# Tree attention on one core: three output stores one block of loads later, six stores ahead of the last rearranging copies, and one late head stored in 116 and 12 rows

## The chip, the core and the metric

The kernel runs on one core of a Trainium2 chip. The core has a matrix engine (TensorE, PE in the profile, with its weight loads as PEld), three engines for elementwise work (VectorE as DVE, ScalarE as ACT, GpSimd as POOL), a synchronisation engine (SyncE, SP) that here only starts transfers, and 16 DMA engines that move data between HBM and the on-chip memories. A transfer is started by an instruction on POOL, SP or ACT; the profile names the queue q0 for POOL's transfers, q1 for SP's and q10 for ACT's. The metric is the device time of one execution in microseconds (us).

## What is computed

Attention over 96 heads (8 batches of 12) of 512 positions by 64 numbers, in which position i may look only at itself and at its ancestors in a binary tree:

```python
    mask = np.zeros((seq, seq))
    for i in range(seq):
        mask[i, i] = 1
        parent = i
        while parent > 0:
            parent = (parent - 1) // 2
            mask[i, parent] = 1
    scores = np.einsum('bhqd,bhkd->bhqk', Q, K) * scale
    scores = scores + (1 - mask) * (-1e9)
    weights = np.exp(scores - np.max(scores, axis=-1, keepdims=True))
    weights = weights / (np.sum(weights, axis=-1, keepdims=True) + 1e-10)
    return np.einsum('bhqk,bhkd->bhqd', weights, V).astype(np.float32)
```

Q, K, V and the result are float32, 12.58 MB each. Three of them are read and one is written.

## The kernel before

Heads are worked on in 48 pairs (`NP`). For pair i the main loop runs steps named by letters: S computes the scores in two parts on PE (lines 601 to 608 and 635 to 646) and their exponentials on ACT (618 and 652); V multiplies pair i-1's exponentials with V on PE (696) and divides by the sums on DVE (733 and 735), which writes one of the output tiles `of`; K and Q turn the next pairs' keys and queries round with PE transposes (507 to 513 and 566 to 572) and copy the result out of PSUM on DVE (521, 525, 577). Copies at line 374 lay V out in the order that the products need; DVE, ACT and POOL share them.

Loads come in blocks of 8 heads for K and Q (`kst`, `qst`, 512 KB as they land in bf16) and of 16 heads for V (`vst`). A V block arrives as "leaves0" and "leaves1" (256 KB each) and "upper" (512 KB). An output tile `of` holds 8 heads, 1 MB in float32; there are ten of them for twelve blocks of heads. In this text k9 or q9 is the load of K's or Q's heads 72 to 79, leaves(5) that of V's heads 80 to 95, and store 24 the store of heads 24 to 31.

All loads and most stores are issued by POOL, in the order of a list that `pool_program` writes out (line 759). `pool(i)` issues, after pair i's steps, as much from the head of the list as `ready` lets through; nothing overtakes, so an instruction of POOL that waits holds up every load and store behind it. Each transfer of POOL also takes one of eight semaphores in turn, and waits until the transfer eight places before it has landed. Besides transfers the list has POOL's own copies of V's rows (`spread_top`, `spread_pool`, line 374), and `lay_beside` (line 448), a copy of a whole K or Q block of heads 80 to 87 or 88 to 95 into another arrangement, from which PE transposes with half as many instructions (lines 507 and 566).

The list before is made by a loop over blocks. A store goes in once it is `BEHIND` (56) heads and a block behind the loads; what is left is stored after the last load. Heads 72 and 73 are stored by SP after pair 38 in pieces of 116 and 12 rows (`store_apart`, line 753); POOL stores the other six of that block. The last four heads are stored by SP and ACT at the end of the program: pair 46's two heads in halves of 64 rows, one head by each engine, then pair 47's, its first head by SP in halves of 64 rows and its second by ACT in one transfer of 128 rows. One row of one head is 1 KB.

Of the kernel before, what the change touches and what calls it, by code (L numbers as in the profile page):

```python
# [10 lines left out]
CODE = 2048.0  # L11
CODE_ROWS = 40
NOUT = 20
BEHIND = 56

# [104 lines left out]
def kernel(  # L120
# [16 lines left out]
    KB, VB = 8, 16  # L137
# [604 lines left out]
    def store(eng, h0, n, step=1, p0=0, p1=P):  # L742
        return eng.dma_start(  # L743
            out=Or[p0:p1, h0:h0 + step * (n - 1) + 1:step, :],
            in_=ofs[h0 // 8][p0:p1, h0 % 8:h0 % 8 + step * (n - 1) + 1:step, :, :].rearrange(
                "p h t d -> p h (t d)"
            ),
        )


    APART, APART_AT, APART_ROWS = 72, 38, 116
# [7 lines left out]
    def pool_program():  # L759

        ops = [
            (load_k, 2, 2), (load_q, 2, 2), (load_v, 0, 4), (load_v, 4, 4),
            (load_k, 4, 2), (load_k, 6, 2), (load_q, 4, 2), (load_k, 8, 4),
            (load_q, 6, 2), (load_q, 8, 4), (load_v, 8, 8), (load_k, 12, 4),
            (load_q, 12, 4), (load_k, 16, 4), (load_rows, 1, "upper"),
            (load_q, 16, 4), (load_rows, 1, "even"), (load_k, 20, 4), (load_rows, 1, "odd"),
            (load_q, 20, 4), (load_k, 24, 8), (load_q, 24, 4), (load_rows, 2, "upper"),
            (load_q, 28, 4), (load_rows, 2, "leaves0", "leaves1"), (load_k, 32, 8), (load_q, 32, 8),
            (load_rows, 3, "upper"),
            (spread_pool, (1, "Z0", 8, 16), (1, "Z1", 8, 16), (1, 6, 8, 16), (1, 9, 8, 16)),  # L770
            (load_q, 40, 8), (load_k, 40, 8), (load_rows, 3, "leaves0", "leaves1"), (load_k, 48, 8),
            (spread_top, 2), (spread_pool, (2, "Z0", 0, 16), (2, "Z1", 0, 16)), (load_q, 48, 8),
            (spread_pool, (2, "X", 0, 16), (2, "M", 0, 16), (2, "D1", 0, 16)), (spread_top, 3, 0, 12),
            (load_rows, 4, "upper"), (spread_top, 3, 12, 16),
        ]
        loaded, stored = 72, 0
        for h in range(56, NH, KB):
            top = [(spread_top, h // VB + 0)] if h % VB == 8 and 4 <= h // VB + 0 < NH // VB else []
            if top:
                top.append((spread_pool, (h // VB, "Z0", 0, 16), (h // VB, "Z1", 0, 16)))  # L780
            ops += [(load_k, h, KB)] + top + [(load_q, h, KB)]
            if h == 64:
                ops.append((
                    spread_pool, *[(3, part, 0, 16) for part in ("Z0", "Z1", "X", "M", "D1")]
                ))
            while loaded < min(h + 32, NH):
                names = ("leaves0", "leaves1") if loaded % VB else ("upper",)
                ops.append((load_rows, loaded // VB) + names)
                loaded += KB
            if top:  # L790
                o = h // VB
                ops.append((spread_pool, *[(o, part, 0, 16) for part in ("X", "M", "D1")]))
            if stored + KB + BEHIND <= h + KB:
                ops.append((store, nc.gpsimd, stored, KB))
                stored += KB
        ops.insert(-1, (lay_beside, "kst", 80 // KB))
        while stored < NH - KB:
            n = 2 if stored == APART else 0
            ops.append((store, nc.gpsimd, stored + n, KB - n))
            if stored == 40:  # L800
                ops.append((lay_beside, "qst", 80 // KB))
            if stored == 64:
                ops += [(lay_beside, "kst", 88 // KB), (lay_beside, "qst", 88 // KB)]
            stored += KB
        ops += [(store, nc.gpsimd, NH - KB + h, 2) for h in (0, 4)]
        return ops

# [57 lines left out]
    def spread_by(copy, table, steady, i):  # L865
# [34 lines left out]
    for i in range(NP + 1):  # L900
        steps = FIRST[i] if i < len(FIRST) else "SVK" if i % 2 else "SVQ"
        if i >= max(FAR, KFAR - 4):
            steps = ("SVK", "SVQ", "SVK", "SQV")[i % 4]
        elif i == FAR - 1:
            steps = "SQVK"
        for step in steps:
            if step == "S" and i < NP:
                scores1(i)
                scores2(i)
            if step == "V" and i >= 1:  # L910
                values(i - 1)
# [12 lines left out]
            if step == "D":  # L924
                spread_by(nc.vector.tensor_copy, BY_VECTOR, STEADY_VECTOR, i)
            if step == "A":
                spread_by(nc.scalar.copy, BY_SCALAR, STEADY_SCALAR, i)
        if "D" not in steps:
            spread_by(nc.vector.tensor_copy, BY_VECTOR, STEADY_VECTOR, i)
        if "A" not in steps:  # L930
            spread_by(nc.scalar.copy, BY_SCALAR, STEADY_SCALAR, i)
        pool(i)
        if i == APART_AT:
            store_apart()
        if i == NP - 1:
# [37 lines left out]
```

## Time and the profile before

| | |
|---|---|
| median of 3 runs | 132.93 us (132.81 to 133.04) |
| the profiled execution, its own time | 132.49 us |
| its span, first to last instruction | 130.7 us |
| busy: PE, DVE, ACT, POOL | 113.7, 105.6, 101.1, 84.4 us |
| read from HBM, written to HBM | 37.94 MB, 12.58 MB |

The profile is of one execution. 1.8 us of its time lie outside the span. A load counts in the DMA rates with the bytes that land (bf16), a store with what it writes (float32), so 200 GB/s of loads and 400 GB/s of stores are about the same traffic at HBM. "Landing" is when the last part of a transfer has reported.

### The profile page before, as it was taken

What the parts mean: (1) busy time and instruction counts of PE and PEld (TensorE: products, weight loads), DVE (VectorE), ACT (ScalarE), POOL (GpSimd) and SP (SyncE); (2) the same over time, 40 slices, a digit from 0 to 9 for tenths busy, and PEclk for the clock granted to TensorE, in tenths of its full rate; (3) what the DMA queues carried; (4) which work ended last, traced back from release to release, by engine and by line L of the source; (5) the groups of instructions that cost most, each with busy time, mean ns of one, the idle gap of its engine ahead of it and who ended that gap; (6) DMA issues with size and microseconds to landing.
All of it is one profiled execution on the core that took longest, in us unless ns stands there. A gap on an engine that the chain in (4) does not pass through costs nothing.

```text
span 130.7 us, 5436 instructions
## 1 busy us (share of the span) xinstructions
PE 113.7 (87%) x2353; PEld 81.0 (62%) x2353; DVE 105.6 (81%) x254; ACT 101.1 (77%) x163; POOL 84.4 (65%) x116
## 2 busy tenths in 40 slices
PE   6688969999799887899998999896999997999940
PEld 2354755766577566677776786674677675776630
DVE  3349779888999998989998998987898997894560
ACT  4179676989779995968987799797689785889930
POOL 6999625354483999995299899953999963202130
PEclk9999999999999999999999999999999999999995
DMA  2999999999999999999999999999999999999984
GB/s 89 248 190 192 201 195 201 201 202 205 201 203 208 208 205 207 208 210 205 207 211 201 283 292 210 270 309 231 338 228 322 257 277 397 402 404 386 382 339 145
DMA packets 26071, 32.25 MB, mean 247 GB/s; under 512 B 1240, under 2 KB 19544, under 8 KB 26048
## 3 DMA queue, kind: packets, MB, share of 16 engines
q0 software_dynamic: 24384, 30.41, 111.4%
q1 hardware_dynamic: 944, 0.91, 2.2%
q10 hardware_dynamic: 720, 0.59, 1.5%
q8 instruction: 18, 0.29, 0.8%
q14 instruction: 5, 0.04, 0.1%
HBM read 37.94 MB, written 12.58 MB: 386 GB/s over the span
## 4 chain that ended last, share of the span: by engine, by line
DVE 29%; DMA 28%; PE 22%; POOL 7%; ACT 6%; issue 4%; ACTq 0%; DVEq 0%; POOLq 0%
DMA vst<-in_V_dram 17%; DMA qst<-in_Q_dram 11%; DVE of L735 9%; PE ob L696 8%; DVE vt L374 6%; PE s L601 3%; DVE qq L577 3%; ACT e L652 3%; DVE rec L733 3%; DVE kk L521 3%; POOL kst L247 2%; PE s L608 2%; DVE kk L525 2%; POOL qst L247 2%; ACT e L618 2%
## 5 line engine op out<-in xcount | busy, mean ns | idle before, releaser
L618 ACT ACTIVATE e<-s 128x1024 bf16<-128x1024 f32 x40 | 40.9, 1024 | 15.0 <-PE s L608 14.6
L696 PE MATMUL ob<-vt,e 128*128 128x65 bf16 (+1 forms) x940 | 37.1, 197 | 2.6 <-DVE of L735 1.0
L696 PEld LDWEIGHTS <-e 128*128 128x128 bf16 (+1 forms) x960 | 30.1, 102 | 9.6 <-DVE of L735 1.9
L374 POOL COPY vt<-vst 32x512 int32<-32x512 int32 (+4 forms) x44 | 32.5, 739 | 4.7 <-PE ob L696 2.5
L652 ACT ACTIVATE e<-s 128x384 bf16<-128x384 f32 x80 | 34.7, 490 | 0.0
L735 DVE TENSOR_TENSOR of<-ob,rec 128x512 f32<-128x512 f32 x47 | 32.5, 691 | 1.6
L374 DVE COPY vt<-vst 32x1024 bf16<-32x1024 bf16 (+5 forms) x47 | 20.9, 445 | 2.8 <-DMA vst<-in_V_dram 1.9
L743 POOL DMA_DIRECT2D out_dram<-of x13 | 11.5, 888 | 12.9 <-DVE of L735 12.4
L733 DVE RECIPROCAL rec<-ob 128x8 f32<-128x8 f32 x47 | 9.5, 202 | 9.9 <-PE ob L696 9.3
L257 POOL DMA_DIRECT2D kst<-in_K_dram x11 | 8.0, 725 | 7.4 <-DMA qst<-in_Q_dram 3.2
L601 PE MATMUL s<-far,codes 40*128 40x512 bf16 x64 | 12.5, 386 | 0.0
L635 PEld LDWEIGHTS <-codes 40*128 40x128 bf16 x80 | 6.2, 94 | 8.7 <-issue 3.9
L614 ACT ACTIVATE e<-s 128x1024 bf16<-128x1024 f32 x8 | 8.2, 1023 | 4.1 <-PE s L608 4.0
L577 DVE COPY qq<-qtp 128x1024 bf16<-128x1024 bf16 x16 | 10.9, 680 | 0.3 <-PE qtp L572 0.3
L635 PE MATMUL s<-far,codes 40*128 40x384 bf16 x64 | 10.7, 324 | 0.4 <-ACT e L652 0.2
L257 POOL DMA_DIRECT2D qst<-in_Q_dram x12 | 8.5, 708 | 3.8 <-DMA vst<-in_V_dram 1.9
L374 ACT COPY vt<-vst 32x512 int32<-32x512 int32 (+3 forms) x19 | 10.4, 545 | 0.4
L608 PE MATMUL s<-qq,kk 64*128 64x512 bf16 x48 | 9.2, 378 | 1.0 <-DVE qq L577 1.0
L646 PEld LDWEIGHTS <-kk 64*128 64x128 bf16 x192 | 8.4, 94 | 2.6
L521 DVE COPY kk<-ktp 128x256 bf16<-128x256 bf16 x24 | 9.0, 414 | 0.7 <-PE ktp L513 0.7
L302 POOL DMA_DIRECT2D vst<-in_V_dram x7 | 5.6, 800 | 6.0 <-DMA vst<-in_V_dram 4.3
L572 PE MATMUL qtp<-ptile,qst 128*64 128x128 bf16 x192 | 7.5, 221 | 1.7 <-DVE qq L577 1.0
(64 smaller groups left out, 178.2 us busy)
## 6 DMA issues: line engine op xcount, KB each, us to landing
out_dram<-of POOLq DMA_DIRECT2D x10, 1024.0 KB, 15.2
kst<-in_K_dram POOLq DMA_DIRECT2D x9, 512.0 KB, 16.5
qst<-in_Q_dram POOLq DMA_DIRECT2D x8, 512.0 KB, 14.8
vst<-in_V_dram POOLq DMA_DIRECT2D x12, 256.0 KB, 13.5
vst<-in_V_dram POOLq DMA_DIRECT2D x6, 512.0 KB, 12.9
qst<-in_Q_dram POOLq DMA_DIRECT2D x6, 256.0 KB, 12.1
kst<-in_K_dram POOLq DMA_DIRECT2D x4, 256.0 KB, 10.3
out_dram<-of POOLq DMA_DIRECT2D x1, 768.0 KB, 13.0
```

The costliest lines, as they stand in the source:

```text
L257: return nc.gpsimd.dma_start(out=kept[b][:, h0 % KB:h0 % KB + n, :, :].rearrange("p (g x) t d -> p g (x t d)", x=x), in_=src[:, h0 // x:(h ...
L374: return copy(out=dst, in_=src)
L521: nc.vector.tensor_copy(out=columns(flat, 32 * unit, (640, 4), (step, 2), (4, 8), (1, 4)), in_=columns(kp, base, (256, 4), (128, 2), (1, 8 ...
L577: nc.vector.tensor_copy(out=qqs[j][:, :, 8 * last:8 * last + 8, :].rearrange("p b u c -> p b (u c)"), in_=quarters,)
L601: nc.tensor.matmul(out=sp[:, a, :], lhsT=(k1code if i < WIDE else k1wide)[64 * a:64 * a + CODE_ROWS, :], rhs=(q1code, q1wide, q1far)[(i >= ...
L608: nc.tensor.matmul(out=sp[:, a, :], lhsT=keys(i, a, TOP), rhs=qTs[i][64 * a:64 * a + 64, :, :].rearrange("p t c -> p (t c)"), start=False, ...
L618: ) if i < WIDE else nc.scalar.activation(
L635: nc.tensor.matmul(out=flat[:, a, :, :].rearrange("p u (t c) -> p u t c", t=4)[:, :, :, 32 // n:], lhsT=k2wide[64 * a:64 * a + CODE_ROWS, ...
L652: nc.scalar.activation(out=e2s[i % NE][:, a, :, 32:128].rearrange("p t (r u) -> p t r u", u=n), in_=flat[:, a, :, :].rearrange("p u (t r) ...
L696: nc.tensor.matmul(out=ob[lo:hi, a, 65 * t:65 * t + 65], lhsT=e[:, a, PLACE[t], lo:hi], rhs=vt[vtile[tile_v][0]][:, head(i, a) % VB, vtile ...
L733: nc.vector.reciprocal(out=rec[:, a:a + n, :, :], in_=o4[:, a:a + n, :, D:D + 1])
L735: nc.vector.tensor_tensor(out=ofs[j][:, h0:h1 + 1:head(i, 1) - head(i, 0), :, :], in0=o4[:, a:a + n, :, 0:D], in1=rec[:, a:a + n, :, :].to ...
```

## The change

The loop over blocks is replaced by a list that is written out, `BEHIND` goes, and SP's store of pair 46's first head is cut differently. Loads, copies and stores are the same ones as before; in POOL's order four things move:

- stores 8, 16 and 24 each come one block of loads later: store 8 after the loads of k9 and q9 and not before them, store 16 after k10 and q10, store 24 after k11, q11, POOL's last copies of V and the two `lay_beside` of heads 80 to 87;
- the load upper(5) comes after k8, q8, POOL's copies for V block 3 and leaves(5), and not ahead of store 0;
- the second `lay_beside` of heads 80 to 87 (of `qst`) follows the first directly, ahead of every store of that stretch;
- stores 24 to 64, six in a row, stand ahead of the two `lay_beside` of heads 88 to 95.

POOL before, from the load upper(5) to that of k9. `of_312` is the output tile of heads 0 to 7, `of_597` of 8 to 15, `of_875` of 16 to 23; `vst_1914` is V block 5, and the `kst` and `qst` rows are k8, q8 and k9:

```order
L302 DMA vst_1914<-in_V_dram 64x16x256
L743 DMA out_0_dram<-of_312 128x8x256
L257 DMA kst_1917<-in_K_dram 128x2x1024
L257 DMA qst_1919<-in_Q_dram 128x2x1024
L374 COPY vt1_1_122<-vst_822 32x32x32 x2
L374 COPY vt1_2_123<-vst_822 32x32x32 x2
L374 COPY vt1_1_122<-vst_822 32x8x2x32
L293 DMA vst_1914<-in_V_dram 32x8x512 x2
L743 DMA out_0_dram<-of_597 128x8x256
L257 DMA kst_1929<-in_K_dram 128x2x1024
```

POOL after, at the same place; V block 5 is `vst_1924` here, k8 and k9 are `kst_1468` and `kst_1928`:

```order
L742 DMA out_0_dram<-of_312 128x8x256
L256 DMA kst_1468<-in_K_dram 128x2x1024
L256 DMA qst_1470<-in_Q_dram 128x2x1024
L373 COPY vt1_1_122<-vst_822 32x32x32 x2
L373 COPY vt1_2_123<-vst_822 32x32x32 x2
L373 COPY vt1_1_122<-vst_822 32x8x2x32
L292 DMA vst_1924<-in_V_dram 32x8x512 x2
L301 DMA vst_1924<-in_V_dram 64x16x256
L256 DMA kst_1928<-in_K_dram 128x2x1024
```

The upper rows of V block 5 have moved from the front to behind the leaves, and the store of heads 8 to 15 (`of_597`) no longer stands between leaves(5) and k9.

POOL before, around the rearranging copies of line 448, from the load of q11 (`qst_2466`) on; `kst_2007` and `qst_2009` are k10 and q10, `kst_2268` is k11, and the output tiles are those of heads 32 to 71 in order:

```order
L257 DMA qst_2466<-in_Q_dram 128x2x1024
L374 COPY vt1_2_123<-vst_1914 32x32x32 x2
L374 COPY vt1_1_122<-vst_1914 32x8x2x32
L448 COPY kst_2536<-kst_2007 128x1024
L743 DMA out_0_dram<-of_1443 128x8x256
L743 DMA out_0_dram<-of_1701 128x8x256
L448 COPY qst_2540<-qst_2009 128x1024
L743 DMA out_0_dram<-of_1984 128x8x256
L743 DMA out_0_dram<-of_2244 128x8x256
L743 DMA out_0_dram<-of_2512 128x8x256
L448 COPY kst_2784<-kst_2268 128x1024
L448 COPY qst_2786<-qst_2466 128x1024
```

POOL after, at the same place; `of_1151` is the output tile of heads 24 to 31:

```order
L256 DMA qst_2465<-in_Q_dram 128x2x1024
L373 COPY vt1_2_123<-vst_1924 32x32x32 x2
L373 COPY vt1_1_122<-vst_1924 32x8x2x32
L447 COPY kst_2535<-kst_2006 128x1024
L447 COPY qst_2537<-qst_2008 128x1024
L742 DMA out_0_dram<-of_1151 128x8x256
L742 DMA out_0_dram<-of_1444 128x8x256
L742 DMA out_0_dram<-of_1711 128x8x256
L742 DMA out_0_dram<-of_1983 128x8x256
L742 DMA out_0_dram<-of_2243 128x8x256
L742 DMA out_0_dram<-of_2511 128x8x256
L447 COPY kst_2784<-kst_2267 128x1024
```

The store of heads 24 to 31 has come down into this stretch, both copies for heads 80 to 87 stand ahead of it, and all six stores stand ahead of the copies for heads 88 to 95.

SP before, its stores: two heads apart, then pair 46's first head and pair 47's first head:

```order
L743 DMA out_0_dram<-of_2769 116x256 x2
L743 DMA out_0_dram<-of_2769 12x256 x2
L743 DMA out_0_dram<-of_3206 64x256 x4
```

SP after:

```order
L742 DMA out_0_dram<-of_2769 116x256 x2
L742 DMA out_0_dram<-of_2769 12x256 x2
L742 DMA out_0_dram<-of_3206 116x256
L742 DMA out_0_dram<-of_3206 12x256
L742 DMA out_0_dram<-of_3206 64x256 x2
```

Pair 46's first head goes out as rows 0 to 115 and rows 116 to 127; ACT's stores and pair 47's stay as they were. The diff, without the lines that only define names:

```diff
-            if stored + KB + BEHIND <= h + KB:
-                ops.append((store, nc.gpsimd, stored, KB))
-                stored += KB
-        ops.insert(-1, (lay_beside, "kst", 80 // KB))
-        while stored < NH - KB:
-            n = 2 if stored == APART else 0
-            ops.append((store, nc.gpsimd, stored + n, KB - n))
-            if stored == 40:
-                ops.append((lay_beside, "qst", 80 // KB))
-            if stored == 64:
-                ops += [(lay_beside, "kst", 88 // KB), (lay_beside, "qst", 88 // KB)]
-            stored += KB
...
+        ops += k7 + q7 + leaves(4) + out(0)
+        ops += k8 + q8 + [(spread_pool, *[(3, part, 0, 16) for part in ("Z0", "Z1", "X", "M", "D1")])]
+        ops += leaves(5) + [(load_rows, 5, "upper")]
+        ops += k9 + tops(4) + q9 + rest(4) + out(8)
+        ops += k10 + q10 + out(16)
+        ops += k11 + tops(5) + q11 + rest(5)
+        ops += [(lay_beside, "kst", 80 // KB), (lay_beside, "qst", 80 // KB)]
+        for h in range(24, 72, KB):
+            ops += out(h)
+        ops += [(lay_beside, "kst", 88 // KB), (lay_beside, "qst", 88 // KB)]
+        for h in range(72, NH - KB, KB):
+            n = 2 if h == APART else 0
+            ops += out(h + n, KB - n)
...
         if i == NP - 1:
-            for p in (0, P // 2):
-                for a, eng in enumerate((nc.sync, nc.scalar)):
-                    store(eng, head(i - 1, a), 1, 1, p, p + P // 2)
+            for part in range(2):
+                for a, (eng, p) in enumerate(((nc.sync, 116), (nc.scalar, P // 2))):
+                    store(eng, head(i - 1, a), 1, 1, *((0, p), (p, P))[part])
```

More of the change, by code (lines that the diff above doesn't have):

```diff
@@ L13 @@
 NOUT = 20
-BEHIND = 56
 UNITS = (
@@ L775, in pool_program @@
         ]
[L776 to L792, printed above, removed]
-            if stored + KB + BEHIND <= h + KB:
-                ops.append((store, nc.gpsimd, stored, KB))
-                stored += KB
@@ L796, in pool_program, with tops @@
-        ops.insert(-1, (lay_beside, "kst", 80 // KB))
-        while stored < NH - KB:
-            n = 2 if stored == APART else 0
-            ops.append((store, nc.gpsimd, stored + n, KB - n))
-            if stored == 40:
-                ops.append((lay_beside, "qst", 80 // KB))
-            if stored == 64:
-                ops += [(lay_beside, "kst", 88 // KB), (lay_beside, "qst", 88 // KB)]
-            stored += KB
+        def tops(o):
+            return [(spread_top, o), (spread_pool, (o, "Z0", 0, 16), (o, "Z1", 0, 16))]
@@ new lines, in rest, with out, leaves, qk @@
+        def rest(o):
+            return [(spread_pool, (o, "X", 0, 16), (o, "M", 0, 16), (o, "D1", 0, 16))]
+        def out(h0, n=KB):
+            return [(store, nc.gpsimd, h0, n)]
+        def leaves(o):
+            return [(load_rows, o, "leaves0", "leaves1")]
+        def qk(h0):
+            return [(load_k, h0, KB)], [(load_q, h0, KB)]
+        k7, q7 = qk(56)
+        k8, q8 = qk(64)
+        k9, q9 = qk(72)
+        k10, q10 = qk(80)
+        k11, q11 = qk(88)
+        ops += k7 + q7 + leaves(4) + out(0)
```

## Prediction

> **What bounds the kernel now.** I read the page's head and its row of DMA slices first:
>
> ```profile
> span 130.7 us, 5436 instructions
> ...
> DMA  2999999999999999999999999999999999999984
> ```
>
> From the second slice to the 38th no slice of the DMA row is below 9: taken together the DMA engines never run out of work. So I read the stretches of the end next, with one of the middle for comparison (columns: stretch, its length, busy time and instructions of PE, PEld, DVE, ACT, POOL, the clock, the DMA engines' share, and what they moved in GB/s):
>
> ```profile
> core 0: us, PE busy (x) PEld busy (x) DVE busy (x) ACT busy (x) POOL busy (x), PEclk, DMA share, GB/s
> ...
> 80.00:90.00 10.00, 9.23 (x212) 6.88 (x211) 8.89 (x20) 8.24 (x14) 6.76 (x8) 1.00 1.13 261
> ...
> 114.00:120.00 6.00, 5.76 (x108) 4.08 (x109) 4.46 (x10) 5.18 (x10) 0.00 (x0) 1.00 1.03 402
> 120.00:124.00 4.00, 3.87 (x84) 2.60 (x80) 1.80 (x4) 3.81 (x7) 0.89 (x1) 1.00 0.96 373
> ...
> 127.00:128.00 1.00, 0.00 (x0) 0.00 (x0) 0.00 (x0) 0.00 (x0) 0.00 (x0) 0.58 0.88 279
> 128.00:129.00 1.00, 0.00 (x0) 0.00 (x0) 0.00 (x0) 0.00 (x0) 0.00 (x0) 0.50 0.88 262
> 129.00:130.00 1.00, 0.00 (x0) 0.00 (x0) 0.00 (x0) 0.00 (x0) 0.00 (x0) 0.50 0.21 67
> ```
>
> Stores run at 402 GB/s while all engines have work, 25.1 per DMA engine. From 120 on the rate falls, though stores are queued: some of the 16 have run dry, others have not. After 127.0 all compute is over and only transfers are left. Which engines have work to the end shows in the POOL stores' issue times (each row was asked for by itself, so each is one store) and, in the same order, their times to landing:
>
> ```profile
> 102.68 1.10 POOL L743 DMA_DIRECT2D out_dram<-of  x1
> ...
> 103.78 0.89 POOL L743 DMA_DIRECT2D out_dram<-of  x1
> ...
> 104.66 0.89 POOL L743 DMA_DIRECT2D out_dram<-of  x1
> ...
> 111.56 0.83 POOL L743 DMA_DIRECT2D out_dram<-of  x1 [1.61 <-DVE of L735]
> ...
> 120.25 0.89 POOL L743 DMA_DIRECT2D out_dram<-of  x1 [7.86 <-DVE of L735]
> ...
> 124.72 0.72 POOL L743 DMA_DIRECT2D out_dram<-of  x1
> ```
>
> ```profile
> out_dram<-of POOLq DMA_DIRECT2D x1, 1024.0 KB, 14.0
> ...
> out_dram<-of POOLq DMA_DIRECT2D x1, 1024.0 KB, 16.3
> ...
> out_dram<-of POOLq DMA_DIRECT2D x1, 1024.0 KB, 18.0
> ...
> out_dram<-of POOLq DMA_DIRECT2D x1, 768.0 KB, 13.0
> ...
> out_dram<-of POOLq DMA_DIRECT2D x1, 1024.0 KB, 6.9
> ...
> out_dram<-of POOLq DMA_DIRECT2D x1, 256.0 KB, 3.8
> ```
>
> Sums: landings at 116.7, 120.1, 122.7, 124.6, 127.2 and 128.5. A landing is that of the last engine's part. From 120.1 on the steps are 2.6, 1.9, 2.6 and 1.3 for 1024, 768, 1024 and 512 KB (two stores of 256), which is 402 GB/s each time (1,049 KB / 402 = 2.61). So the engine that lands last works without a gap at full pace up to 128.5, while the total rate says that others already idle. The step before, 116.7 to 120.1, is 3.4, that is 0.8 longer than a store needs. In that store something made other engines the last ones.
>
> **The 116-row pieces.** SP's queue q1 had two of them in flight then, 256 KB with their 12-row pieces. Its rows for 108 to 114 and 114 to 120.7, and for 127 to 128, where it carries 64-row pieces:
>
> ```profile
> q1 hardware_dynamic: 156, 0.14, 6.7%
> ...
> q1 hardware_dynamic: 132, 0.12, 5.2%
> ...
> q1 hardware_dynamic: 129, 0.11, 34.6%
> ```
>
> In 116-row pieces the queue moved 0.26 MB in 12.7 us (20 GB/s), busy for about 6% of 16 engines, one engine's worth. In 64-row pieces it moved 0.11 MB in 1 us (110 GB/s) at 35%, five times as much, although POOL's and ACT's queues were also at work. So a 116-row piece is carried by a few engines: between a fifth and a quarter of them by that ratio. I take a quarter, four engines with 29 rows each. An even spread over 16 would have lengthened each of the stores of that time by 20/402, 0.13 us; one step of 0.8 in a single store and none after fits four engines that were ahead, took 58 KB each (2.3 us at 25.1 GB/s), used up their lead and came out last.
>
> The Trainium skill, "DMA: Bandwidth & Descriptors", section "Why a DMA increments its semaphore by 16 and not by 1", gives the rule: a transfer from SP or ACT uses the largest number of engines up to 16 that divides its slowest dimension, and the lowest-numbered ones. By it 116 rows go to four engines, 12 rows to twelve and 64 rows to all, and the sum below would be the same to a tenth; the rows above agree with four, and no row here names the engines.
>
> **The change, part by part.**
>
> Stores 8, 16 and 24 behind k9/q9, k10/q10, k11/q11, and upper(5) behind k8/q8: each load has 1 MB (or upper(5)'s 512 KB, the same traffic at HBM) less ahead of it in q0 and lands 2.6 us earlier. What that is worth to compute is PE's wait for loads between 78 and 96, and no more:
>
> ```profile
> PE ktp L513 <- DMA kst<-in_K_dram: 1.2, 2, 1.0
> PE qtp L572 <- DMA qst<-in_Q_dram: 0.7, 2, 0.5
> ```
>
> 1.9 us at most. DVE, 8.9 us busy in ten there, keeps some, so I take 1.3. The last division then ends 1.3 earlier than the 126.97 below. But bytes are not saved: an engine that is busy to 128.5 without a gap has the same work in another order. For the end this part is worth 0 by itself, up to -1.3 if the issue of the last stores were the bound.
>
> ```profile
> 126.55 0.42 DVE L735 TENSOR_TENSOR of<-s,rec 128x256 f32<-128x256 f32 x1
> ...
> 125.67 2.46 SPq L743 DMA_DIRECT2D out_dram<-of  x4
> ...
> out_dram<-of SPq DMA_DIRECT2D x1, 64.0 KB, 3.0
> ```
>
> SP's last issue ends at 128.13 and begins some 0.6 earlier (2.46 / 4), at 127.5; the last bytes move soon after 129 (67 GB/s in that row). A piece of 64 rows took up to 3.0 us (SP's first). So the path of the issues and the drain of the last engine end close together today; the first moves forward by 1.3, the second does not.
>
> Late stores: does anything wait for them? Of the ten output tiles two are used again, those of stores 0 and 8, for heads 80 to 95. Store 8 goes ahead of k10 in q0, and heads 80 on are computed from k10. Nothing.
>
> Upper(5) later, with its issue, its landing and its first reader:
>
> ```profile
> 58.73 0.83 POOL L302 DMA_DIRECT2D vst<-in_V_dram  x1
> ...
> vst<-in_V_dram POOLq DMA_DIRECT2D x1, 512.0 KB, 17.1
> ...
> 90.23 4.87 POOL L374 COPY vt<-vst 32x512 int32<-32x512 int32 x6 [2.49 <-PE ob L696]
> ```
>
> It landed at 75.8. Store 0, k8, q8 and leaves(5) now go ahead of it, four times 2.6, so 86.2. POOL's copies that read it began at 90.2 and would begin near 89: almost 3 us of cover, 0. Without it q11, which POOL issues behind these copies, would come late, and the copies for heads 88 to 95 next.
>
> Both copies for heads 80 to 87 first, then six stores, then the copies for heads 88 to 95:
>
> ```profile
> 101.70 1.05 POOL L448 COPY qst<-qst 128x1024 int32<-128x1024 int32 x1
> 102.68 2.86 POOL L743 DMA_DIRECT2D out_dram<-of  x3
> 106.43 1.04 POOL L448 COPY kst<-kst 128x1024 int32<-128x1024 int32 x1 [0.89 <-DMA kst<-in_K_dram]
> 108.91 1.04 POOL L448 COPY qst<-qst 128x1024 int32<-128x1024 int32 x1 [1.43 <-DMA qst<-in_Q_dram]
> ```
>
> Q's copy ended at 102.75 with two stores ahead of it; without them (0.95 each, 2.86 / 3) it ends at 100.9, or a little before. Six stores take POOL to 106.6, the two copies to 108.7. They waited for k11 and q11 until 106.4 and 108.9; those now land 2.6 earlier, so the stores, not the loads, set them. PE needs the two results one after the other:
>
> ```profile
> 110.13 0.61 PE L507 MATMUL ktp<-ptile,kst 128*128 128x128 bf16 x8
> ```
>
> With compute 1.3 ahead that is 108.8 for K and about 111 for Q. K's copy is done at 107.6. Cost 0, with 1.2 us of cover; without it every later pair would slip. q0 meanwhile has q11 until 106.3 and stores 24 and on behind it, so no gap opens there.
>
> Pair 46's first head in 116 and 12 rows: before, 64 + 64 rows, 8 KB on each of 16 engines. After, 29 + 1 KB on each of four. Those four gain 22 KB, the others lose 7 or 8. At 25.1 GB/s per engine that is +0.88 us. With a fifth of the engines (39 KB each) it is +1.24. At the rate of 128 to 129 (262 GB/s over 88% of 16, 18.6 per engine) it is +1.18. From below: if the four were not the last, the end would be 8 KB earlier, -0.32. I take +0.95, near the 402 GB/s row, since the last landings kept that pace to the end.
>
> Sum: 0 + 0 + 0.95. The profiled execution's 132.49 becomes 133.44 (span 131.65); the median of the runs lies 0.44 above that execution, so 132.93 + 0.95 = 133.9.
>
> **Rivals.** A difference of 0.2%, 0.27 us, is about what a measurement of this kernel can tell from none.
>
> (a) The four engines are not the last. Place: the last landing. Price -0.32, 132.6. It decides if their lead over the others at 128.5 is 0.9 us or more. For it: the fall of the rate from 120 on shows engines with a lead, and the issue path, 1.3 earlier, would no longer stand in the way. Against it: the step of 0.8 at 120.1. The same page, section "Latency and other measured facts", says that engines 7 and 15 are usually slower; if those were the last, this is the case, but no row here shows single engines.
>
> (b) The issue of the last stores bounds the end, not the drain. Then compute's 1.3 us comes through: 131.6. Against it: the landings without a gap, and 279 and 262 GB/s after the last compute.
>
> (c) Both cancel: the four had half a microsecond in hand, and the result lies within 0.27 of 132.9.
>
> (d) Slower still: the 116 rows start late in their queue. SP issued the first 116-row store at 104.3, and in the stretch 104 to 108 the only queue with bytes was q0:
>
> ```profile
> 104.30 0.27 SPq L743 DMA_DIRECT2D out_dram<-of  x1
> ...
> q0 software_dynamic: 434, 1.09, 110.2%
> ```
>
> If the 29 rows per engine run alone at half pace, +1.8, or POOL's six stores delay the copies for heads 88 to 95, 2 us and more. 134.7.
>
> **Chances.** Forecast (+0.5 to +1.3) 0.62, (d) 0.08, (c) 0.12, (a) 0.11, (b) 0.07. Slower by over 0.2%: 0.70. Same: 0.12. Faster: 0.18. The forecast's own range is 133.4 to 134.2; for 8 in 10 it reaches down to (a) without most of it and all of (b), and up into (d): 132.4 to 134.6.
>
> **What would show it.** The span is about 131.7; the last microsecond before the end has some 100 GB/s (four engines at 25) where 67 stood in 129 to 130, and q1 rather than q10 carries it. PE's waits for `kst` and `qst` between 78 and 96 fall under 0.6, and the last division ends between 125 and 126. The copies for heads 88 to 95 follow a store directly, without a wait for DMA. Wrong would be: a DMA rate of zero within 129.5 of the start, which is (a) or (b); PE waiting for `kst` or `qst` on line 507 or 566, which is (d).

## The result and the profile after

The changed kernel took 133.74 us (median of 6 runs, 133.34 to 133.80), the kernel before 132.87 us beside it (6 runs, 132.60 to 133.04). The ratio is 1.0063, with a 95% interval of 1.0046 to 1.0080: 0.84 us slower, between 0.61 and 1.06. The forecast was 133.9.

The page of the changed kernel: its head, the row of the DMA slices, and the group of DVE's copies of V (before: 20.9 us, 445 ns each).

```profile
span 132.0 us, 5436 instructions
...
DMA  3999999999999999999999999999999999999982
...
L373 DVE COPY vt<-vst 32x1024 bf16<-32x1024 bf16 (+5 forms) x47 | 23.1, 492 | 2.9 <-DMA vst<-in_V_dram 2.1
```

The DMA engines are as full as before. What differs is the end. The stretches of the end of the changed kernel, with the columns of the prediction's table:

```profile
114.00:120.00 6.00, 5.76 (x111) 4.08 (x107) 4.46 (x11) 5.18 (x10) 0.00 (x0) 1.00 1.03 402
120.00:124.00 4.00, 3.87 (x80) 2.60 (x78) 1.84 (x5) 3.81 (x7) 0.89 (x1) 1.00 0.98 383
...
127.00:128.00 1.00, 0.00 (x0) 0.00 (x0) 0.06 (x1) 0.00 (x0) 0.00 (x0) 1.00 0.78 214
128.00:129.00 1.00, 0.00 (x0) 0.00 (x0) 0.00 (x0) 0.00 (x0) 0.00 (x0) 0.52 0.96 263
129.00:130.00 1.00, 0.00 (x0) 0.00 (x0) 0.00 (x0) 0.00 (x0) 0.00 (x0) 0.50 0.55 181
130.00:131.00 1.00, 0.00 (x0) 0.00 (x0) 0.00 (x0) 0.00 (x0) 0.00 (x0) 0.50 0.09 30
```

The rate while all engines have work is the same 402 GB/s. In 127 to 128 it is lower than before (214 where 279 stood), and the bytes come afterwards: 181 GB/s in 129 to 130 where 67 stood, and 30 beyond 130, where the kernel before had moved its last. Who moves these bytes stands in the queues' rows for 129 to 131 (packets, MB, share of 16 engines), in the changed kernel:

```profile
q1 hardware_dynamic: 130, 0.10, 16.0%
q10 hardware_dynamic: 127, 0.11, 15.9%
```

and in the kernel before:

```profile
q1 hardware_dynamic: 65, 0.05, 7.9%
q10 hardware_dynamic: 21, 0.02, 2.4%
```

Only SP's stores (q1) were cut differently, but ACT's (q10) are late as well. ACT's two halves of pair 46's second head take longer from issue to landing, after:

```profile
out_dram<-of ACTq DMA_DIRECT2D x1, 64.0 KB, 4.4
...
out_dram<-of ACTq DMA_DIRECT2D x1, 64.0 KB, 4.2
```

where before they took

```profile
out_dram<-of ACTq DMA_DIRECT2D x1, 64.0 KB, 3.1
...
out_dram<-of ACTq DMA_DIRECT2D x1, 64.0 KB, 2.9
```

A landing is that of the last engine's part, and one number hides the others. The trace also keeps the single steps in which a store's semaphore (the counter that tells when it has landed) rises. They show how many engines carry a piece: a piece of 64, 112 or 128 rows rises in 16 separate steps, one of 116 rows in four, one of 12 rows in twelve and one of 127 rows in one, and what is missing to 16 comes all at once near the issue. Read as one step per engine, the last store of the program, SP's last 64 rows, tells when each of the 16 was done (us from the start of the span; the span ends 0.9 after the last one in every row):

| kernel (the lower ones are the experiments below) | the twelve that end first | the last four |
|---|---|---|
| before | 129.40 to 129.70 | 129.70, 129.71, 129.77, 129.81 |
| changed | 129.44 to 130.05 | 130.27, 130.47, 130.91, 131.06 |
| e1_order | 128.57 to 129.33 | 129.49, 129.76, 129.87, 130.23 |
| e2_rows | 128.93 to 129.43 | 129.94, 130.16, 130.32, 130.62 |
| e3_rows112 | 129.63 to 129.99 | 130.03, 130.05, 130.09, 130.33 |
| e4_rows_both | 130.23 to 130.70 | 131.73, 131.89, 131.90, 132.51 |
| e5_apart_even | 127.69 to 128.84 | 128.95, 129.06, 130.02, 130.19 |
| e6_before_apart_even | 129.86 to 130.21 | 130.23, 130.26, 130.51, 131.27 |
| e7_stores_back | 130.49 to 130.87 | 130.89, 130.89, 130.89, 130.96 |
| e10_rows127 | 131.22 to 131.71 | 131.80, 131.93, 132.36, 135.46 |

Before, all 16 end within 0.4 us. In the changed kernel the first twelve end up to 0.35 us later than before, and the last four 0.6 to 1.25 us later. ACT's halves land late because these four carry their sixteenths of them too: of the first half twelve parts are in by 128.90 and four come at 129.43 to 130.15.

Compute's part: in the changed kernel PE's list of waits between 78 and 96 holds no load any more (columns: us in total, times, longest). It is headed by

```profile
PE s L607 <- DVE qq L576: 0.4, 1, 0.4
PE ob L695 <- DVE of L734: 0.2, 1, 0.2
```

and POOL's stores, its copies for heads 88 to 95, and the last division stand in the changed kernel's timeline (start, length) as

```profile
101.19 5.31 POOL L742 DMA_DIRECT2D out_dram<-of  x6
...
106.49 1.05 POOL L447 COPY kst<-kst 128x1024 int32<-128x1024 int32 x1
107.47 1.05 POOL L447 COPY qst<-qst 128x1024 int32<-128x1024 int32 x1
...
126.63 0.42 DVE L734 TENSOR_TENSOR of<-s,rec 128x256 f32<-128x256 f32 x1
```

The copies follow the stores without a wait. But the last division is where it was before (126.55): in this execution the 1.9 us that PE no longer waits for loads did not reach the end of compute.

### The profile page after: what moved, and what is told of

Same layout as the page of the kernel before. It is cut to its first block, busy times and chain, and to the rows that moved or that the text cites. A ratio compares the mean times of both kernels' runs of the same rounds, so it can differ in the third digit from the quotient of the medians.

```text
span 132.0 us, 5436 instructions
## 1 busy us (share of the span) xinstructions
PE 114.3 (87%) x2353; PEld 81.0 (61%) x2353; DVE 107.5 (81%) x254; ACT 101.1 (77%) x163; POOL 84.4 (64%) x116
## 4 chain that ended last, share of the span: by engine, by line
DVE 39%; PE 24%; DMA 19%; POOL 6%; ACT 4%; issue 3%; ACTq 0%; POOLq 0%
DVE of L734 12%; DMA qst<-in_Q_dram 12%; PE ob L695 9%; DMA vst<-in_V_dram 7%; DVE vt L373 7%; DVE kk L520 5%; DVE qq L576 5%; DVE kk L524 5%; PE s L600 3%; DVE rec L732 3%; PE s L607 2%; POOL kst L246 2%; POOL qst L246 2%; ACT e L617 2%; ACT e L651 2%
## 5 line engine op out<-in xcount | busy, mean ns | idle before, releaser
L617 ACT ACTIVATE e<-s 128x1024 bf16<-128x1024 f32 x40 | 40.9, 1024 | 15.0 <-PE s L607 14.6
L373 DVE COPY vt<-vst 32x1024 bf16<-32x1024 bf16 (+5 forms) x47 | 23.1, 492 | 2.9 <-DMA vst<-in_V_dram 2.1
L645 PE MATMUL s<-qq,kk 64*128 64x160 bf16 (+1 forms) x192 | 8.9, 208 | 0.0
```

The source lines that it names most:

```text
L373: return copy(out=dst, in_=src)
L617: ) if i < WIDE else nc.scalar.activation(
L645: nc.tensor.matmul(out=flat[:, a, :, lo:hi], lhsT=keys(i, a, WTILE2[t]), rhs=qT[64 * a:64 * a + 64, :, lo:hi], start=False, stop=t == 1, s ...
```

## The experiments

The theory, as the prediction had it: the end is set by the DMA engines, the one that lands last; the uneven cut puts 22 KB more on each of four of them and costs all of the loss; the new order on POOL is worth nothing at the end. The first rival was that both parts contribute; later ones were that a lead of the four engines, or the end of compute, decides. Each kernel was timed in turns with the kernel before on the same chip. All of them, with the ratio to the kernel before and its 95% interval, and the difference worked out from it and the median of before on that chip (132.75 us for e1 to e4, 133.0 for e5 to e8, 133.11 for e9 to e12). On the second and third chip the kernel before was itself spread over more than 1.4 us, and plain medians give other differences there (+0.72, +0.56 and +0.61 for e5, e6 and e7; -0.32, -0.42 and -0.18 for e8, e9 and e12), so that a tenth or two decides nothing between these rows:

| kernel | median us | ratio | difference, us |
|---|---|---|---|
| e1_order: new order on POOL, halves of 64 rows | 133.23 | 1.0036 [1.0016, 1.0056] | +0.48 |
| e2_rows: order before, 116 + 12 rows | 133.58 | 1.0064 [1.0046, 1.0083] | +0.85 |
| e3_rows112: order before, 112 + 16 rows | 132.84 | 1.0004 [0.9986, 1.0021] | +0.05 |
| e4_rows_both: order before, both heads of pair 46 in 116 + 12 | 135.21 | 1.0186 [1.0161, 1.0210] | +2.47 |
| e5_apart_even: changed kernel, heads 72 and 73 in 112 + 16 | 133.72 | 1.0043 [1.0013, 1.0072] | +0.57 |
| e6_before_apart_even: kernel before, heads 72 and 73 in 112 + 16 | 133.56 | 1.0032 [1.0005, 1.0060] | +0.43 |
| e7_stores_back: stores 8 to 24 and upper(5) moved, second copy behind three stores | 133.61 | 1.0031 [0.9999, 1.0064] | +0.41 |
| e8_copies_first: only the second copy moved | 132.68 | 0.9961 [0.9936, 0.9986] | -0.52 |
| e9_first_92: e8 and heads 72 and 73 in 92 + 36 | 132.69 | 0.9975 [0.9949, 1.0001] | -0.33 |
| e10_rows127: order before, 127 + 1 rows | 138.34 | 1.0395 [1.0347, 1.0444] | +5.26 |
| e11_less_compute: kernel before with less copying | 132.83 | 0.9982 [0.9956, 1.0009] | -0.24 |
| e12_copies_first_again: e8 a second time | 132.93 | 0.9979 [0.9953, 1.0006] | -0.28 |

**One part alone: the order (e1_order) and the rows (e2_rows).** e1 is the changed kernel with pair 46 in halves again; e2 is the kernel before with the uneven cut.

```diff
 e1_order, against the changed kernel
-            for part in range(2):
-                for a, (eng, p) in enumerate(((nc.sync, 116), (nc.scalar, P // 2))):
-                    store(eng, head(i - 1, a), 1, 1, *((0, p), (p, P))[part])
+            for p in (0, P // 2):
+                for a, eng in enumerate((nc.sync, nc.scalar)):
+                    store(eng, head(i - 1, a), 1, 1, p, p + P // 2)
 e2_rows, against the kernel before: the same lines the other way round
```

> POOL's new order alone, pair 46's first head in two halves of 64 rows as before. Drain theory (the engine that drains last has the same work in any order): ratio to before 1.000, between 0.998 and 1.001. Rival (the path of the last issues bounds the end and late stores help): 0.990. Rival (the order itself costs, through vector copies that take longer beside POOL's copies: the mean of line 373's DVE copies went from 445 to 492 ns in the changed kernel): 1.003 or more.

> The old order, with pair 46's first head stored in 116 and 12 rows. Drain theory: all of the loss, ratio 1.0065 (0.87 us), between 1.005 and 1.008, and the last landings show q1 alive for about a microsecond after the rest. Rival (the cut costs nothing and the order costs): 1.000.

The rows alone cost 0.85 us [0.61, 1.10], as much as the whole change. In e2's trace the end is the expected one in part: four engines are done 0.5 to 1.2 us after the twelfth (129.94 to 130.62 against 129.43), but SP's queue is not the only one alive then, since the four have their share of ACT's stores left as well. The order alone, which was to cost nothing, cost 0.48 us [0.21, 0.74]. The two don't seem to add up: 0.48 + 0.85 is 1.33, and the whole change cost 0.84. The gap of 0.49 is about as large as the three intervals together leave room for. It fits an end that is a maximum over engines and not a sum of delays. The end of e1_order, in the same columns:

```profile
127.00:128.00 1.00, 0.00 (x0) 0.00 (x0) 0.00 (x0) 0.00 (x0) 0.00 (x0) 0.50 0.98 329
128.00:129.00 1.00, 0.00 (x0) 0.00 (x0) 0.00 (x0) 0.00 (x0) 0.00 (x0) 0.50 0.64 215
129.00:130.00 1.00, 0.00 (x0) 0.00 (x0) 0.00 (x0) 0.00 (x0) 0.00 (x0) 0.50 0.12 41
```

and its last division, with its last but one and its last POOL store:

```profile
125.55 0.42 DVE L734 TENSOR_TENSOR of<-s,rec 128x256 f32<-128x256 f32 x1
...
119.25 0.89 POOL L742 DMA_DIRECT2D out_dram<-of  x1 [7.87 <-DVE of L734]
...
123.72 0.72 POOL L742 DMA_DIRECT2D out_dram<-of  x1
```

```profile
out_dram<-of POOLq DMA_DIRECT2D x1, 1024.0 KB, 8.3
...
out_dram<-of POOLq DMA_DIRECT2D x1, 256.0 KB, 5.2
```

Here compute does end 1.0 us earlier, the stores are issued 1.0 earlier, and more bytes move in 127 to 128 (329 where 279 stood). Yet the landings, 119.25 + 8.3 = 127.55 and 123.72 + 5.2 = 128.9, are 0.4 later than before (127.2 and 128.5), while most engines are done earlier: twelve of the 16 by 129.33, where before they took until 129.70, and the last at 130.23 against 129.81. So a few engines fell behind somewhere. Which, and why, the trace does not tell.

**Is it the number of rows or the unequal cut? (e3_rows112, e10_rows127, e4_rows_both)** In all three the order is that of the kernel before and only the cut of pair 46 differs.

```diff
-                for a, eng in enumerate((nc.sync, nc.scalar)):
+                for a, (eng, p) in enumerate(((nc.sync, 112), (nc.scalar, P // 2))):   e3_rows112
+                for a, (eng, p) in enumerate(((nc.sync, 127), (nc.scalar, P // 2))):   e10_rows127
+                for a, (eng, p) in enumerate(((nc.sync, 116), (nc.scalar, 116))):      e4_rows_both
```

> The old order, with that head stored in 112 and 16 rows: as unequal as 116 and 12, but both numbers divide by 16. Theory that a piece is carried by as many engines as divide its rows: 8 KB on each of 16 engines as with the halves, ratio 1.000. Rival (a large first piece ahead of a small one in SP's queue costs, however it is spread): 1.005 or more.

> The old order, with pair 46's first head in 127 rows and 1 row. Theory of divisors (127 has none up to 16 but 1): one engine carries 127 KB and 1 KB where it had 8, 120 KB more, 4.8 us at 25.1 GB/s if that engine was among the last: ratio 1.033 to 1.040; at the 18.6 GB/s of the last stretch 6.5 us, 1.049. Rival (pieces that do not divide by 16 go through four engines or so): 1.007.

> The old order, with both heads of pair 46 stored in 116 and 12 rows, SP's and ACT's. Drain theory: the same four engines get 22 KB more twice, 1.76 us at 25.1 GB/s, ratio 1.013. Rival (SP's and ACT's pieces go through different engines): 1.0065, as with one head.

112 + 16 rows cost 0.05 us [-0.19, 0.28], 116 + 12 cost 0.85, 127 + 1 cost 5.26 [4.62, 5.91]. So a large first piece costs nothing by itself. It costs what lands on its engines: 112 and 16 are both divisible by 16, 116 by 4 and no larger number up to 16, 127 by none. By the pace of 25.1 GB/s, 22 KB more are 0.90 us and 120 KB more (127 and 1 less the 8 that an engine had) are 4.9. (A row has 1,024 bytes; the prediction's 0.88 and the expectations' 1.76 and 4.8 count a KB as 1,000.) The Trainium skill, "DMA: Bandwidth & Descriptors", section "Why a DMA increments its semaphore by 16 and not by 1", says the same of 127 rows, that they put everything on one engine. The trace agrees; the end of e10_rows127:

```profile
127.00:128.00 1.00, 0.00 (x0) 0.00 (x0) 0.11 (x1) 0.00 (x0) 0.00 (x0) 1.00 0.64 187
...
133.00:134.00 1.00, 0.00 (x0) 0.00 (x0) 0.00 (x0) 0.00 (x0) 0.00 (x0) 0.50 0.07 25
134.00:135.00 1.00, 0.00 (x0) 0.00 (x0) 0.00 (x0) 0.00 (x0) 0.00 (x0) 0.50 0.07 23
```

7% of 16 is 1.1 engines, and that one alone moves 25 and 23 GB/s, about its share when all 16 are busy. In the table one engine ends at 135.46, 3.1 us after the next.

Two heads instead of one (e4) missed. By the bytes it was to be 44 KB on each of the four engines, 1.80 us; it took 2.47 [2.14, 2.79]. Its end, and the issues of its last stores by SP and ACT:

```profile
127.00:128.00 1.00, 0.00 (x0) 0.00 (x0) 0.22 (x1) 0.00 (x0) 0.00 (x0) 1.00 0.55 138
128.00:129.00 1.00, 0.00 (x0) 0.00 (x0) 0.00 (x0) 0.00 (x0) 0.00 (x0) 1.00 0.47 102
129.00:130.00 1.00, 0.00 (x0) 0.00 (x0) 0.00 (x0) 0.00 (x0) 0.00 (x0) 0.80 0.89 225
130.00:131.00 1.00, 0.00 (x0) 0.00 (x0) 0.00 (x0) 0.00 (x0) 0.00 (x0) 0.50 0.39 130
```

```profile
125.91 2.09 SPq L743 DMA_DIRECT2D out_dram<-of  x4
...
125.92 1.77 ACTq L743 DMA_DIRECT2D out_dram<-of  x3
```

All stores are issued by 128.0, pair 47's among them, which go in 64 and 128 rows and so over all 16 engines. Still half of the engines' time in 127 to 129 is idle (138 and 102 GB/s), and the wide pieces' bytes come in 129 to 130. The wide pieces stand in the same two queues behind the narrow ones. The table agrees: the twelve engines that carry nothing of the 116 rows end at 130.23 to 130.70, up to a microsecond later than before, though they have 14 to 16 KB less and the last issue (begun at 127.29, before at 127.53) was no later. So a narrow piece loads its own engines and also delays the pieces behind it on the others. In the changed kernel these twelve end 2.3 to 2.9 us after the last issue began (127.15), in the kernel before 1.9 to 2.2 and in e4 2.9 to 3.4, so the effect is there too, but smaller. What in the queue holds them was not tried apart.

**How much lead have the four engines? (e5_apart_even, e6_before_apart_even)** Heads 72 and 73 go out in 116 + 12 rows in the kernel before and after. With 112 + 16 they are spread over all engines: each of the four gets 44 KB less, the others 14 to 16 KB more.

```diff
-    APART, APART_AT, APART_ROWS = 72, 38, 116
+    APART, APART_AT, APART_ROWS = 72, 38, 112
```

> The changed kernel with heads 72 and 73 cut at row 112 and not at row 116, so that these 256 KB go through all 16 engines; pair 46's head stays at 116 and 12. Drain theory (the same four engines carry every 116-row piece, and what they carry in all sets the end): they lose 44 KB each (60 less 16), 1.8 us, and are no longer last; the others gain 14 to 16 KB, 0.6 us. Ratio to before about 0.997 to 1.001, and in any case 0.5 us or more faster than the changed kernel. Rival (only the last microseconds count, where the piece of pair 46 is alone): 1.0065, no better than the changed kernel.

> The kernel before with heads 72 and 73 cut at row 112: every piece goes through all 16 engines. Drain theory with the four engines 0.2 to 0.3 us later than the rest before: ratio 0.997 to 0.999, limited by the path of the last issues. Rival (the uneven cut of heads 72 and 73 uses up a lead that these four have, and the others are late without it): 1.002 or more, since the others get 14 to 16 KB more.

Both went against the theory that the four engines are last and would gladly be rid of that load; e6 came out as its rival had it. In the changed kernel it gave back no more than 0.27 us (0.84 to 0.57), well inside the intervals; in the kernel before it made the time longer by 0.43 us [0.07, 0.80]. In e6's trace (taken of the longest of its 12 runs) the end holds more bytes, 226 GB/s where 67 stood in 129 to 130:

```profile
129.00:130.00 1.00, 0.00 (x0) 0.00 (x0) 0.00 (x0) 0.00 (x0) 0.00 (x0) 0.50 0.69 226
```

though the last division also came 0.5 later there (127.09), so the row alone would not decide it. Read together with e2: 22 KB more on the four made the end 0.85 later, and at 25.1 GB/s they are 0.90, so the four had no lead worth a name at the end of the kernel before. 14 to 16 KB more on the other twelve are 0.57 to 0.65, and made it 0.43 later; if these bytes did it, the twelve were ahead by some 0.2. The table has the same for the kernel before: all 16 end within 0.4 us.

But the table also shows something that bytes do not explain. In e5 (the trace is of its shortest run) fourteen engines are done by 129.06, earlier than any was in the kernel before, so the load did leave the four; two others end a whole microsecond later. In e6 fifteen are done by 130.51 and one at 131.27. Such a lag stands in POOL's stores already and begins in a single one of them. Two stores of e6 that follow each other, issue and time to landing, and between the two landings the queue that the profile calls instruction (packets, MB, share of 16 engines):

```profile
103.17 0.89 POOL L743 DMA_DIRECT2D out_dram<-of  x1
...
104.05 0.89 POOL L743 DMA_DIRECT2D out_dram<-of  x1
```

```profile
out_dram<-of POOLq DMA_DIRECT2D x1, 1024.0 KB, 14.6
...
out_dram<-of POOLq DMA_DIRECT2D x1, 1024.0 KB, 17.5
...
q8 instruction: 1, 0.02, 1.7%
```

The landings are 117.8 and 121.6, 3.8 us apart where a store needs 2.6. In e5 two are 3.7 apart, at 114.4 and 118.1, again with one packet of q8 between them. Such a packet has 16 KB and took 1.0 us, about what the late engine lost. That the engine which carries it falls back by it fits, but is weak evidence, since the queue moves one packet about every 6 us, and was not tried. So whether e6's 0.43 us are the 14 to 16 KB or the luck of these packets stays open.

**Which part of the order? (e7_stores_back, e8_copies_first, e12_copies_first_again, e9_first_92)** e7 has stores 8, 16 and 24 and upper(5) where the change has them and the second copy behind store 40, as it was, but with store 24 now ahead of it too, so behind three stores and not two; e8 and e12, one kernel, are the kernel before with only the second copy moved directly behind the first; e9 is e8 with a lighter load on the four engines (92 rows are again 4 times 23, 36 are 12 times 3).

```diff
 e7_stores_back, against the changed kernel (with pair 46 in halves)
-        ops += [(lay_beside, "kst", 80 // KB), (lay_beside, "qst", 80 // KB)]
+        ops += [(lay_beside, "kst", 80 // KB)]
...
             ops += out(h)
+            if h == 40:
+                ops += [(lay_beside, "qst", 80 // KB)]
 e8_copies_first and e12_copies_first_again, against the kernel before
-        ops.insert(-1, (lay_beside, "kst", 80 // KB))
+        ops[-1:-1] = [(lay_beside, name, 80 // KB) for name in ("kst", "qst")]
...
-            if stored == 40:
-                ops.append((lay_beside, "qst", 80 // KB))
 e9_first_92, besides e8's lines
-    APART, APART_AT, APART_ROWS = 72, 38, 116
+    APART, APART_AT, APART_ROWS = 72, 38, 92
```

> Stores 8, 16 and 24 one block of loads later and upper(5) behind leaves(5), but the copies of line 448 where they were among the stores, and pair 46's first head in halves. Theory 1 (the late stores themselves cost, at the drain): 1.0036 as for the whole order. Theory 2 (the copies put together ahead of six stores cost): 1.000. Compute should end about 1 us earlier in either.

> The kernel before with the second copy of heads 80 to 87 directly behind the first, so that the five stores 32 to 64 stand in a row ahead of the copies for heads 88 to 95; stores 8, 16 and 24 and upper(5) where they were, halves of 64 rows. Theory 1 (the late stores cost): 1.000. Theory 2 (the copies together cost): 1.0036.

> The same kernel as e8_copies_first, beside other runs of the kernel before, since those were spread widely there (132.5 to 134.7). If the order of the copies is worth something: 0.996 to 0.998. If the gain was the spread of the kernel before: 0.999 to 1.001.

> Copies first (the order of e8_copies_first) and heads 72 and 73 cut at row 92: by divisors 92 rows go to four engines and 36 to twelve, so the four carry 52 KB and not 60, eight others 6 and not 2, the last four nothing. If the four engines are still the last by 0.2 to 0.6 us, the end comes 0.2 to 0.3 us before that of the copies alone: ratio to before about 0.995 to 0.998. Rival (all engines end together already): as e12_copies_first_again, or 0.1% above it.

e7 is +0.41 us, about what the whole order costs (+0.48), and the interval, -0.01 to 0.85, just reaches zero. But it does not measure the late stores alone. With three stores ahead of it the second copy comes too late for PE, a wait that neither the kernel before nor e1 has; PE's longest wait between 100 and 112, and the last division:

```profile
PE qtp L565 <- POOL qst L447: 1.6, 1, 1.6
```

```profile
127.73 0.42 DVE L734 TENSOR_TENSOR of<-s,rec 128x256 f32<-128x256 f32 x1
```

Compute was expected to end about 1 us earlier and ended 1.2 later; the span, 131.9, is 1.2 longer too, and all 16 engines end together (130.49 to 130.96). So in this execution the loss is a late end of compute that came through, and no engine that drains late. The copies put first cost nothing: e8 and e12 are 0.52 and 0.28 us faster, and only the first of the two intervals stays below 1. So the two copies may be worth 0.2 to 0.4%, which is not settled, and which part of the order costs e1's 0.48 us is open. e9 doesn't differ from e8 and e12. No version here was clearly shown to beat the kernel before.

**Does compute's end matter? (e11_less_compute)** The kernel before without some copying:

```diff
+        if o >= 4 and copy != nc.scalar.copy:
+            return None
```

> The kernel before without the copies of V's blocks 4 and 5 on DVE and POOL (line 374, heads 64 to 95; ACT's stay): those heads are then multiplied with older values of V, every transfer stays. DVE and POOL lose some 10 and 20 us of work, and the last division should come 1 us or more earlier. Drain theory: ratio 0.996 to 1.000, the end does not follow. Rival (the path of the last issues): the end follows the last division, 0.990 or less.

0.24 us faster, with an interval that holds zero; but the last division came only 0.3 earlier (126.25), so this run could hardly have told. Better evidence lies in the profiles of all kernels, one execution each: the start of the last division, against the span.

| order on POOL | last division starts | span |
|---|---|---|
| before: before, e2, e3, e4, e6, e10, e11 | 126.55, 126.17, 127.16, 126.80, 127.09, 126.69, 126.25 | 130.7, 131.5, 131.2, 133.4, 132.2, 136.4, 130.9 |
| copies first: e8, e9, e12 | 126.39, 126.38, 126.81 | 130.9, 130.6, 131.1 |
| changed: after, e1, e5 | 126.63, 125.55, 124.67 | 132.0, 131.1, 131.1 |
| late stores, second copy behind three: e7 | 127.73 | 131.9 |

The changed order's mean is 125.6 against 126.7 with the order before, 1.1 earlier. With e1 1.0 and e5 1.9 us earlier than the kernel before, the span is 0.4 longer in both: an earlier end of compute is not passed on. A later one is: e3's is 0.6 later and its span 0.5 longer, e7's 1.2 and 1.2. From the start of the last division to the end of the span it is 4.0 to 4.2 us in the kernel before, e3, e7 and e9, and in no execution less. So two bounds stand side by side at the end, the path of the last issues and the slowest DMA engine, and whichever comes later counts.

## Why the prediction was right, and where not

**The DMA engines bound the end.** Right, and shown. Cutting one late 128 KB store differently moved the time by 0, 0.85 and 5.26 us as its engines' load did; in e2 and in the changed kernel four engines are done last; and an end of compute that was 1.0 and 1.9 us earlier moved nothing forward. Rival (b), by which an earlier end of compute comes through, falls with the last of these. That the path of the issues and the drain "end close together" was right as well: an end of compute 1.2 us later did come through (e7).

**"The four gain 22 KB, the others lose 7 or 8": +0.88, taken as +0.95.** Right: e2 measured 0.85 [0.61, 1.10], and with 112 rows the cost is gone. (By the ratio that the prediction worked with, 20 to 110 GB/s, it would have been under a fifth of the engines, three; that it is four shows in the trace, where the 116-row piece reports in four steps.) The end at full pace was also right, since an engine that works alone keeps 23 to 25 GB/s; rival (d)'s half pace did not occur. Rival (a), a lead of 0.9 us, falls too: the four had none.

**"In that store something made other engines the last ones."** The step of 0.8 at 120.1, the sign by which the prediction held the four engines to be last, does not show that. With even pieces for heads 72 and 73 such a step is still there and larger (3.8 between two landings in e6, 3.7 in e5). In the kernel before, as there, the queue called instruction moved a packet between the two landings (116.7 to 120.1), which may have held up one engine:

```profile
q8 instruction: 1, 0.02, 1.9%
```

That the four came out with no lead is shown by e2 and the table; how they lost it is not.

**What the end would look like.** Span 132.0 for 131.65. The step "carried by q1 rather than q10" was half wrong. The picture was of four engines working alone at 100 GB/s at the end. The four are there, but in the trace 55% of 16 engines are busy in 129 to 130, at 181 GB/s, since the other twelve end at 129.44 to 130.05, and q10 carries as much of it as q1, since the four have their share of ACT's stores left too. The narrow piece also held up the wide ones behind it, an effect that the sum did not have. With one head it cost nothing that could be measured in the time; with two (e4) it cost 0.7 us beyond the bytes, 2.47 for 1.80.

**Stores one block back and upper(5): "for the end this part is worth 0".** The loads came earlier, k9 and q9 by 2.8 us and those of heads 80 to 95 by 1.9 to 2.0 (2.6 predicted for each), upper(5) landed at 86.0 (86.2), and PE's waits for `kst` and `qst` are gone. The step "the last division then ends 1.3 earlier" was right over the three profiles with that order, 1.1, and wrong in the changed kernel's own one, 126.63. In that execution DVE's copies of V took 2.2 us more than before. One stretch shows how: the three such DVE copies between 62 and 70, first before, then after (ns least/median/most, first and last start):

```profile
L374 DVE COPY vt<-vst x3: 416/419/689, 62.3 to 66.8; 32x1024 bf16<-32x1024 bf16 x3
```

```profile
L373 DVE COPY vt<-vst x3: 415/685/1062, 62.0 to 67.2; 32x1024 bf16<-32x1024 bf16 x3
```

The copies are the same; in the changed kernel the slowest lies inside POOL's own copies of V:

```profile
64.25 5.17 POOL L373 COPY vt<-vst 32x1024 int32<-32x1024 int32 x5
```

The Trainium skill, "SBUF — State Buffer", section "SBUF: two separate sides", says that DVE and GpSimd share a pair of ports which one of them holds for a whole instruction while the other is blocked; 1062 ns beside POOL's copies for 415 without them agrees with it. That this is what kept the division late is argued and not shown: in e1 and e5, with the same order, these copies took 21.8 and 21.9 us in all, 23.1 in the changed kernel.

**The order costs 0.** This is the step that failed: alone it cost 0.48 us [0.21, 0.74] (e1). The argument was that an engine that is busy without a gap has the same work in another order. The bytes are indeed the same, but they need not end balanced: in e1 a few engines ended up to 0.4 later while twelve were done earlier. In the changed kernel this does not show on top of the rows' 0.85, which fits an end where only the latest engine counts. So the total came out right with one term too small, and that is luck: had the two losses added, it would have been 1.33, just above the forecast's own range. Of the order's parts, the row of stores behind both copies did no harm (e8, e12). Stores 8, 16, 24 and upper(5) were not tried alone, since e7's loss comes with a wait of PE that the change does not have. Why the order makes some engines later stays open.

**Late stores, upper(5)'s cover, the copies for heads 88 to 95.** As predicted: POOL issued the stores up to 106.5 and the copies at once behind them, with no wait for a load, and PE waits for none of it.

## What to carry to other kernels

When every DMA engine works to the end, count bytes per engine and not per transfer: a late piece of 112 rows is spread over all 16, one of 116 rows lands on four and one of 127 on one, and such a piece costs at least those engines' extra bytes at their single pace (25 GB/s here). Effects on such an end need not add, as the slowest engine alone counts, so measure each part alone and together. Where two bounds stand side by side, relieving one shows nothing and delaying either shows in full: e1's earlier end of compute was lost, e7's later one was not. Look for such a new wait in an experiment's own profile before you read its time as an answer. And a single profile can hide a gain of 1 us in compute: look at several executions before saying that a step did not happen.

## What was not expected of the hardware

- Pieces over all 16 engines waited behind narrow pieces of the same queue, though issued: 138 and 102 GB/s for 2 us in e4, with half of the engines' time idle.
- Single engines fell back by about 1 us in one store (e5, e6), and each time the queue called instruction moved a packet of 16 KB in that stretch. That the packet is the cause is not shown.
- One DMA engine alone moves 23 to 25 GB/s in packets of 1 KB, the same as its share of 402 GB/s over 16 (e10). A narrow piece doesn't speed up when its neighbours stop.
- With 127 + 1 rows the issue itself was slower: SP's four issues at the end took 4.07 us, against 2.46 before, and 2.53 of them went into that of the piece of one row. With 116 + 12 rows they took 2.11 us in the changed kernel.

```profile
125.81 4.07 SPq L743 DMA_DIRECT2D out_dram<-of  x4
```
